# Five pieces instead of three in half-size slots: the down weights of an expert stage's first round

## The chip, the cores and the metric

The kernel runs on one core of a Trainium2 chip. What counts is the device time of one execution in microseconds, taken as the median of several runs. TensorE multiplies matrices, VectorE and ScalarE work on their results, GpSimd does small things, and SyncE (SP) issues the loads from the chip's memory.

## What is computed

The program runs a whole small network on 256 tokens of width 1024 in float32: first two layers of attention and a mixture of experts, then two layers of gated feed-forward blocks around an mLSTM and a Mamba-2 mixer. The change lies in the mixture of experts, which runs once in each of the first two layers. Of the reference, this is what matters:

```python
def _hier_moe(x, w_group, b_group, w_expert, b_expert, w1, w3, w2):
    ...
    order = jnp.argsort(expert_id)        # 16 experts, two of them for each token
    ...
    def expert_block(args):
        xb, e = args
        h = jax.nn.silu(xb @ w1[e]) * (xb @ w3[e])
        return h @ w2[e]

    ys = lax.map(expert_block, (xs, chunk_expert)).reshape(n_slots, d)
    ys = ys * slot_gate[:, None].astype(ys.dtype)
    return jax.ops.segment_sum(ys, slot_tok, num_segments=n_tok + 1)[:n_tok]
```

`w1` and `w3` are 1024 x 512 for each expert, `w2` is 512 x 1024. All 16 experts' weights are loaded, about 100 MB for each layer.

## The kernel before

**Rounds.** The 16 experts are worked in seven rounds (`ROUNDS`: 2, 2, 4, 1, 2, 3 and 2 experts). The first four experts have fixed numbers. The others are taken in the order of how many tokens chose them; `place_sorted` (L1070 to L1091) finds that order on VectorE with two scratch tiles, `flp` and `flx`, writes the expert numbers to `who` (L1090), and SP reads each of them with a TENSOR_LOAD (L1091) before the loads that need it. In round p, `up` multiplies the tokens that `dispatch` gathered into `xe` by `w1` and `w3` (lines "w,xe"), then `h` is the gated result; `down(p)` transposes it to `hT` and multiplies by `w2` (lines "w,hT" or "wh,hT"), and the results, scaled to `yh` and `yl`, are added up (lines "yh,CT" and "yl,CT"). `up(p + 1)` is written ahead of `down(p)`.

**Pieces and slots.** Each expert's weights come in 12 pieces of 512 KB, four each of `w1`, `w3` and `w2`. The generator `experts` (L936) hands them out in the order in which they are used, and every piece takes a slot in the core's memory with `take` and issues its load on SP: L269 for `w1` and `w3` (through `load_w2`), L258 for `w2` (through `load_w`). There are 37 whole slots (`N_UNIT`) and 16 half ones (`N_HALF`). Slots of one size stand in a line: `give` puts a slot at the line's end when the code is through with it, `take` takes the first, both in the order in which the code is written. So a piece's slot, and whoever used that slot last, are fixed when the program is built. The load then has to wait until that last user is done.

**The half slots.** The first `IN_HALVES` pieces of round 0's `w2` don't take one whole slot but two half ones, with a load of 256 KB for each (L955 to L960); `w[0]` holds columns 0 to 511 and `w[1]` the others. In `down`, a product takes the half that it needs:

```python
if name == "w2" and r == 0 and 2 * i + c < IN_HALVES:
    w = [self.take([512], "wh") for _ in range(2)]
    for j in range(2):
        self.nc.sync.dma_start(w[j], A[name][l, c, k * P:(k + 1) * P, j * 512:(j + 1) * 512])
    yield w
else:
    yield piece()
```

Round 0 has experts 0 and 1, and their `w2` pieces alternate: piece 1 is expert 0's first quarter of rows, piece 2 expert 1's, piece 3 expert 0's second quarter, and so on to piece 8. The half slots are also used by `h`, `flp` and other small tiles.

**What sets the order.** The code is written once; a scheduler then places each engine's instructions, by its own estimate of their times. Each engine works through its own list in order, and an instruction that waits holds everything behind it on its engine. SP issues all weight loads of the stage, so a load that waits for its slot holds the loads behind it. Eight loads can be on their way at a time (each takes one of eight semaphores in turn, and waits for the one eight places before).

Of the kernel before, what the change touches and what calls it, by code (L numbers as in the profile page):

```python
# [33 lines left out]
LL0, LL1 = True, True  # L34
KEEP = 14
OVER_UNITS = 6
IN_HALVES = 3
FIXED = 4


# [94 lines left out]
class K:  # L135
# [800 lines left out]
    def experts(self, l):  # L936
# [11 lines left out]
        for r in range(len(ROUNDS) + 1):  # L948
            for name, r, kt, n in (("w1", r, KT, 512), ("w3", r, KT, 512), ("w2", r - 1, 4, D)):
# [3 lines left out]
                for i, pieces in enumerate(zip(*(load(at(name, e), kt) for e in ROUNDS[r]))):  # L953
                    for c, (k, _, piece) in enumerate(pieces):
                        if name == "w2" and r == 0 and 2 * i + c < IN_HALVES:  # L955
                            w = [self.take([512], "wh") for _ in range(2)]
# [1062 lines left out]
```

## Time and profile before

| | us |
|---|---|
| three runs | 2154.83, 2161.49, 2166.03 |
| their median | 2161.49 |
| the profiled execution | 2156.63 |
| its span in the trace | 2154.9 |

| engine | busy, share of the span |
|---|---|
| TensorE | 93% |
| VectorE | 57% |
| ScalarE | 39% |
| GpSimd | 3% |
| transfers (16 engines) | 68.4% |

The profile shows one execution. Its page cuts the span into forty slices of 53.9 us each. An answer on a stretch gives the instructions in order of time, the busy time by engine, or what each engine waited for; L12 is line 12 of the kernel, and times are counted from the start of the span. TensorE's times are partly modelled, so a busy TensorE is not one at its peak. In layer 0 the expert stage lies at about 250 to 470 us, in layer 1 at about 710 to 930.

### The profile page before, as it was taken

Reading aid. Unit: us, or ns where it says so; the run is one execution under the profiler, and the core shown is the slowest. Engines: PE = TensorE matmul, PEld = TensorE weight load, DVE = VectorE, ACT = ScalarE, POOL = GpSimd, SP = SyncE. Lnnn points to the kernel's source line nnn. Section 1 sums busy time; section 2 is a strip of 40 time slices with the busy share of each in tenths; the row PEclk is TensorE's granted clock in tenths of the full one; section 3 lists DMA queues with packets and bytes.
Section 4 is the critical chain, followed back from the end, with each engine's and each line's share of the span. In section 5 each row is a group of like instructions: output and inputs, shape, how many; then the busy total and the mean of one; then the engine's idle time right before and its main releaser. Section 6 shows DMA issues by size and latency. Waiting matters only on the chain.

```text
span 2154.9 us, 28260 instructions
## 1 busy us (share of the span) xinstructions
PE 2009.5 (93%) x10417; PEld 1463.1 (68%) x10417; DVE 1226.0 (57%) x2049; ACT 834.2 (39%) x1359; POOL 63.4 (3%) x108
## 2 busy tenths in 40 slices
PE   7998899989997999979998979999999898998998
PEld 6866543338776443257786867777778797876887
DVE  5876411137776311177657776677667578655544
ACT  5543100024443100054334554345444456745442
POOL 1000000010000000000000000000000000000000
PEclk9998899999998999989998989999999999999999
DMA  6854799986755999968847746874786343334662
GB/s 226 318 160 150 278 410 411 411 335 226 256 176 193 364 409 410 410 207 272 270 161 262 254 147 203 275 261 150 252 281 219 110 129 117 104 136 143 188 209 82
DMA packets 214232, 515.85 MB, mean 239 GB/s; under 512 B 23562, under 2 KB 36936, under 8 KB 214088
## 3 DMA queue, kind: packets, MB, share of 16 engines
q1 hardware_dynamic: 214088, 513.98, 68.4%
q8 instruction: 84, 1.38, 0.3%
q14 instruction: 60, 0.49, 0.1%
HBM read 512.87 MB, written 1.05 MB: 238 GB/s over the span
## 4 chain that ended last, share of the span: by engine, by line
PE 45%; DMA 4%; DVE 4%; ACT 2%; issue 1%; POOL 0%; SPq 0%; DVEq 0%; POOLq 0%; ACTq 0%
PE ps L200 39%; PE ps L122 4%; DMA w<-in_ffn_w_dram 2%; DVE lo L293 2%; PE ps L204 1%; DMA w<-in_mb_w_in_dram 1%; DMA adaw<-in_ada_w_dram 1%; ACT hi L290 1%; DMA w<-in_ml_w_in_dram 1%; DVE xTm L393 0%; DVE lo L297 0%; ACT xTm L395 0%; DVE xTl L398 0%; PE ps L1411 0%; DVE adac L1447 0%
## 5 line engine op out<-in xcount | busy, mean ns | idle before, releaser
L200 PE MATMUL ps<-hi,xTh 128*128 128x512 f32 (+3 forms) x1632 | 641.7, 397 | 38.4 <-ACT xTh L397 24.0
L200 PE MATMUL ps<-hi,xTl 128*128 128x512 f32 (+3 forms) x1632 | 636.3, 390 | 7.5 <-DVE xTl L398 7.2
L293 DVE TENSOR_TENSOR lo<-w,hi 128x1024 fp32r<-128x1024 f32 (+2 forms) x458 | 482.0, 1074 | 271.1 <-ACT hi L290 261.5
L290 ACT CAST hi<-w 128x1024 fp32r<-128x1024 f32 (+2 forms) x458 | 416.3, 931 | 511.4 <-DMA w<-in_ffn_w_dram 331.4
L200 PE MATMUL ps<-lo,xTh 128*128 128x512 f32 (+3 forms) x1632 | 611.1, 387 | 0.9 <-DVE lo L293 0.6
L200 PEld LDWEIGHTS ps<-hi,xTh 128*128 128x128 f32 x1632 | 315.6, 194 | 112.6 <-ACT xTh L397 29.8
L200 PEld LDWEIGHTS ps<-hi,xTl 128*128 128x128 f32 x1632 | 316.8, 194 | 76.9 <-DVE xTl L398 13.6
L200 PEld LDWEIGHTS ps<-lo,xTh 128*128 128x128 f32 x1632 | 313.2, 192 | 66.2 <-DVE lo L293 2.0
L200 PE MATMUL ps<-w,xe 128*32 128x512 f32 (+2 forms) x1088 | 222.8, 597 | 1.7 <-DMA w<-in_w_dram 1.5
L1447 DVE SCALAR_TENSOR_TENSOR adac<-adaw,cact,adac 128x512 f32<-128x512 f32 x252 | 187.4, 748 | 13.8 <-DMA adaw<-in_ada_w_dram 9.8
L200 PEld LDWEIGHTS ps<-w,xe 128*32 128x32 f32 (+2 forms) x1088 | 65.5, 124 | 131.0 <-issue 110.4
L200 PE MATMUL ps<-w,hT 128*32 128x512 f32 (+2 forms) x520 | 132.8, 599 | 0.0
L122 PE MATMUL ps<-xTh,hi 128*128 128x256 f32 x384 | 112.4, 294 | 7.3 <-DVE dr L559 3.5
L122 PE MATMUL ps<-xTh,lo 128*128 128x256 f32 x384 | 111.3, 290 | 0.4 <-DVE lo L293 0.4
L122 PE MATMUL ps<-xTl,hi 128*128 128x256 f32 x384 | 109.9, 288 | 0.0
L1206 DVE TENSOR_TENSOR h<-h,ps 128x512 f32<-128x512 f32 (+1 forms) x14 | 9.6, 687 | 144.9 <-PE ps L200 143.7
L1228 ACT ACTIVATE yh<-ps,gs 128x512 fp32r<-128x512 f32 (+1 forms) x28 | 18.9, 686 | 186.0 <-PE ps L200 185.5
L200 PEld LDWEIGHTS ps<-w,hT 128*32 128x32 f32 (+2 forms) x520 | 38.0, 123 | 72.4 <-issue 59.4
L122 PEld LDWEIGHTS ps<-xTh,hi 128*128 128x128 f32 x384 | 75.2, 197 | 8.9 <-issue 4.0
L397 ACT CAST xTh<-ps 128x512 fp32r<-128x512 f32 (+1 forms) x84 | 42.7, 523 | 92.8 <-PE ps L204 89.7
L1229 DVE SCALAR_TENSOR_TENSOR yl<-ps,gs,yh 128x512 fp32r<-128x512 f32 (+1 forms) x28 | 20.7, 749 | 101.5 <-ACT yh L1228 101.0
L122 PEld LDWEIGHTS ps<-xTh,lo 128*128 128x128 f32 x384 | 75.4, 196 | 0.8 <-DVE lo L293 0.5
(350 smaller groups left out, 2014.2 us busy)
## 6 DMA issues: line engine op xcount, KB each, us to landing
w<-in_w_dram SPq DMA_DIRECT2D x378, 512.0 KB, 10.1
w<-in_ffn_w_dram SPq DMA_DIRECT2D x264, 512.0 KB, 4.6
adaw<-in_ada_w_dram SPq DMA_DIRECT2D x144, 512.0 KB, 4.9
w<-in_w_in_dram SPq DMA_DIRECT2D x60, 512.0 KB, 6.2
w<-in_mb_w_in_dram SPq DMA_DIRECT2D x40, 512.0 KB, 4.2
w<-in_ml_w_in_dram SPq DMA_DIRECT2D x24, 512.0 KB, 5.7
w<-in_w_out_dram SPq DMA_DIRECT2D x16, 512.0 KB, 5.7
w<-in_mb_w_out_dram SPq DMA_DIRECT2D x16, 512.0 KB, 3.3
```

What stands on the lines that cost most here:

```text
L122: self.k.nc.tensor.matmul(out, lhsT, rhs, start=not self.started, stop=stop)
L200: self.nc.tensor.matmul(out, lhsT, rhs, start=start, stop=stop)
L204: self.nc.tensor.transpose(out, in_, self.ident[:n, :n])
L290: self.nc.scalar.copy(hi[:, k], w[:, k])
L293: self.nc.vector.tensor_sub(lo[:, k], w[:, k], hi[:, k].bitcast(F32))
L397: first = nc.scalar.copy(h, ps)
L1206: V.tensor_mul(h[:m], h[:m], hp[1][:m])
L1228: nc.scalar.mul(yh[:m], py[n][:m], g)
L1229: V.scalar_tensor_tensor(yl[:m], py[n][:m], g, yh[:m].bitcast(F32), OP.mult, OP.subtract)
L1447: nc.vector.scalar_tensor_tensor(prev, wt[:, k], cc, prev, OP.mult, OP.add)
```

## The change

One number is changed: `IN_HALVES` is 5. So pieces 4 and 5 of round 0's `w2`, in each of the two layers, take two half slots and two loads of 256 KB each instead of one whole slot and one load.

```diff
 KEEP = 14
 OVER_UNITS = 6
-IN_HALVES = 3
+IN_HALVES = 5
 FIXED = 4
```

By the code's own lines of slots, in layer 0 piece 4's halves now take the slots that `flp` and round 0's `h` had, and piece 5's halves take those of piece 1 (the tiles `wh_2548` and `wh_2549` below). Pieces 6 to 8 and all later ones take other whole slots than before, two places further back in the line. The scheduler places the loads and products anew. In the rows below, a number behind a name tells tiles of one name apart, "x2" stands for two alike, and the names in brackets are semaphores: DMAHW is one of the eight for loads, PE, DVE (VectorE) and Activation (ScalarE) stand for the engine waited for.

**SP ahead of the expert numbers**, layer 0. Before (pieces 4 to 8 are the whole tiles `w_2564`, `w_2570`, `w_2572`, `w_2578` and `w_2580`):

```order
L258 DMA w_2564<-in_w2_dram 128x1024 [waits DMAHW4_49,PE_49]
L258 DMA w_2570<-in_w2_dram 128x1024 [waits DMAHW5_49,PE_49]
L258 DMA w_2578<-in_w2_dram 128x1024 [waits DMAHW6_49,PE_49]
L258 DMA w_2580<-in_w2_dram 128x1024 [waits DMAHW7_49,PE_49]
L258 DMA w_2572<-in_w2_dram 128x1024 [waits DMAHW0_49,DVE_49]
L1091 TENSOR_LOAD who_2368 [waits DVE_49]
L1091 ISA x2
L1091 TENSOR_LOAD who_2368
```

After:

```order
L258 DMA w_2576<-in_w2_dram 128x1024 [waits DMAHW4_49,PE_49]
L258 DMA w_2582<-in_w2_dram 128x1024 [waits DMAHW5_49,PE_49]
L958 DMA wh_2564<-in_w2_dram 128x512 [waits DMAHW6_49,DVE_49]
L258 DMA w_2584<-in_w2_dram 128x1024 [waits DMAHW7_49,DVE_49]
L1091 TENSOR_LOAD who_2368 [waits DVE_49]
L1091 ISA x2
L1091 TENSOR_LOAD who_2368
L1091 ISA x2
```

Pieces 6 to 8 are `w_2576`, `w_2582` and `w_2584` now, and `wh_2564` is piece 4's first half. Two whole loads less and one half more stand ahead of the reads of `who`. After the rows shown, five reads in all stand ahead of the first load of round 2, where four did.

**SP at the end of the loads of round 2's `w1` and `w3`**, layer 0, some 28 loads later. The `w2` pieces here belong to round 1. Before:

```order
L269 DMA w_2800<-in_w3_dram 128x1024 [waits DMAHW6_49,PE_49]
L269 ISA
L269 DMA w_2802<-in_w3_dram 128x1024 [waits DMAHW7_49,PE_49]
L269 ISA
L269 DMA w_2804<-in_w3_dram 128x1024 [waits DMAHW0_49,PE_49]
L258 DMA w_2826<-in_w2_dram 128x1024 [waits DMAHW1_49,PE_49]
L258 DMA w_2828<-in_w2_dram 128x1024 [waits DMAHW2_49,PE_49]
L258 DMA w_2834<-in_w2_dram 128x1024 [waits DMAHW3_49,PE_49]
L258 DMA w_2836<-in_w2_dram 128x1024 [waits DMAHW4_49,PE_49]
```

After:

```order
L958 DMA wh_2565<-in_w2_dram 128x512 [waits DMAHW2_49,DVE_49,PE_49]
L269 ISA
L269 DMA w_2790<-in_w3_dram 128x1024 [waits DMAHW3_49,Activation_49]
L269 ISA
L269 DMA w_2792<-in_w3_dram 128x1024 [waits DMAHW4_49,Activation_49]
L958 DMA wh_2572<-in_w2_dram 128x512 [waits DMAHW5_49,PE_49]
L958 DMA wh_2573<-in_w2_dram 128x512 [waits DMAHW6_49,PE_49]
L269 ISA
L269 DMA w_2802<-in_w3_dram 128x1024 [waits DMAHW7_49,PE_49]
L269 ISA
L269 DMA w_2804<-in_w3_dram 128x1024 [waits DMAHW0_49,PE_49]
```

Three half loads stand here now: piece 4's second half and, two loads later, both halves of piece 5, which wait for TensorE. The load behind them, `w_2802`, takes the slot of `w_2576`, which is piece 6.

**TensorE in the first down step**, layer 0: products of round 0's `hT` with the pieces. Before, from the fourth product on:

```order
L200 MATMUL ps_2547<-wh_2553,hT_2544 64x512
L200 MATMUL ps_2546<-wh_2560,hT_2544 64x512
L200 MATMUL ps_2546<-w_2564,hT_2544 64x512
L200 MATMUL ps_2547<-wh_2561,hT_2544 64x512
L200 MATMUL ps_2547<-w_2564,hT_2544 64x512
L200 MATMUL ps_2546<-w_2570,hT_2544 64x512
L200 MATMUL ps_2546<-w_2572,hT_2544 64x512
L200 MATMUL ps_2547<-w_2570,hT_2544 64x512
L200 MATMUL ps_2547<-w_2572,hT_2544 64x512
L200 MATMUL ps_2546<-w_2578,hT_2544 64x512
L200 MATMUL ps_2546<-w_2580,hT_2544 64x512
L200 MATMUL ps_2547<-w_2578,hT_2544 64x512
```

After, from piece 5 on (the product with piece 4's second half, `wh_2565`, stands seven rows above; ahead of that stand 12 rows of dispatch and the transposes of the next round's `h`, most of which stood behind this down step before):

```order
L122 MATMUL ps_2925<-R_2184,Ds_2259 128x2
L200 MATMUL ps_2546<-wh_2572,hT_2544 64x512
L200 MATMUL ps_2546<-w_2576,hT_2544 64x512
L200 MATMUL ps_2546<-w_2582,hT_2544 64x512
L200 MATMUL ps_2546<-w_2584,hT_2544 64x512
L204 MATMUL ps_2937<-cf_73,Ds_2259 64x128
L204 MATMUL ps_2937<-cf_73,Ds_2259 128x128 x2
L200 MATMUL ps_2547<-wh_2573,hT_2544 64x512
L200 MATMUL ps_2547<-w_2576,hT_2544 64x512
L200 MATMUL ps_2547<-w_2582,hT_2544 64x512
L200 MATMUL ps_2547<-w_2584,hT_2544 64x512
L200 MATMUL ps_2297<-yh_2590,CT_2448 128x512
```

The products with pieces 6 to 8 (`w_2576`, `w_2582`, `w_2584`) stand half behind `wh_2572` and half behind `wh_2573`, so the slot of `w_2576` is free one product after the last half of piece 5 is used. In layer 1 the two lists are changed in the same places.

On SP the order differs besides only among the loads of the mLSTM's weights and of the modulation's (`adaw`), where some change places.

## Rows read from the trace of the kernel before

**Rows 1.** The page's forty slices of 53.9 us: GB/s that the transfer engines moved.

```profile
GB/s 226 318 160 150 278 410 411 411 335 226 256 176 193 364 409 410 410 207 272 270 161 262 254 147 203 275 261 150 252 281 219 110 129 117 104 136 143 188 209 82
```

**Rows 2.** Both stages' windows: engines' busy us (count), PEclk, DMA share, GB/s.

```profile
255.00:260.00 5.00, 5.00 (x28) 2.35 (x28) 3.09 (x8) 0.00 (x0) 0.00 (x0) 1.00 1.01 336
260.00:265.00 5.00, 5.00 (x26) 1.72 (x24) 3.89 (x17) 0.32 (x1) 0.00 (x0) 1.00 0.94 340
265.00:270.00 5.00, 5.00 (x34) 2.87 (x30) 1.29 (x5) 2.15 (x3) 0.00 (x0) 1.00 0.94 332
...
420.00:460.00 40.00, 39.03 (x154) 10.94 (x156) 3.36 (x5) 1.97 (x3) 3.12 (x6) 1.00 1.03 411
...
850.00:900.00 50.00, 48.85 (x248) 15.55 (x248) 6.54 (x11) 2.83 (x5) 0.00 (x0) 1.00 1.03 410
```

**Rows 3.** SP in order, 250 to 330: start, duration, load, count.

```profile
254.68 6.56 SPq L258 DMA_DIRECT2D w<-in_w_dram  x5
264.07 35.23 SPq L269 DMA_DIRECT2D w<-in_w_dram  x32
300.19 9.29 SPq L258 DMA_DIRECT2D w<-in_w_dram  x8
310.49 9.08 SPq L269 DMA_DIRECT2D w<-in_w_dram  x8
```

**Rows 4.** What SP waited for, 300 to 466: total, times, longest, us.

```profile
SPq L269 <- DMA w<-in_w_dram: 48.2, 64, 1.4
SPq L258 <- DMA w<-in_w_dram: 45.4, 61, 1.4
```

**Rows 5.** What TensorE's weight loads waited for, 400 to 466.

```profile
PEld ps L200 <- DMA w<-in_w_dram: 9.6, 21, 1.2
PEld ps L200 <- ACT yh L1228: 2.9, 4, 0.8
```

**Rows 6.** VectorE in order, 255 to 263: the sorting's last steps.

```profile
258.74 1.06 DVE L1086 TENSOR_TENSOR flx<-R,flp 128x864 f32<-128x864 f32 x1
...
260.92 0.16 DVE L1090 CAST who<-R 1x12 int32<-1x12 f32 x1
```

**Rows 7.** SP's reads of the expert numbers: count, ns, first and last start.

```profile
L1091 SPq TENSOR_LOAD <-who x12: 263/268/469, 261.3 to 275.9; - x12
```

**Rows 8.** The page's list of loads: count, KB, median us to landing.

```profile
w<-in_w_dram SPq DMA_DIRECT2D x378, 512.0 KB, 10.1
```

**Rows 9.** TensorE in order, 266 to 300: first down step, round 2's start.

```profile
286.30 2.33 PE L200 MATMUL ps<-wh,hT 128*64 128x512 f32 x9
...
289.37 4.03 PE L200 MATMUL ps<-w,hT 128*64 128x512 f32 x17
293.32 0.51 PE L122 MATMUL ps<-Ds,xh 128*128 128x256 f32 x2
...
295.35 0.62 PE L200 MATMUL ps<-yh,CT 128*128 128x512 f32 x2
...
296.37 1.90 PE L200 MATMUL ps<-w,xe 128*32 128x512 f32 x10
```

**Rows 10.** Loads into an empty queue, issued at 216.6 and 235.7.

```profile
DMA to landing us min/median/max: 3.5/3.5/3.5
...
DMA to landing us min/median/max: 3.6/3.6/3.6
```

**Rows 11.** SP in order in layer 1, 705 to 790.

```profile
712.21 4.44 SPq L258 DMA_DIRECT2D w<-in_w_dram  x5
...
756.17 9.92 SPq L258 DMA_DIRECT2D w<-in_w_dram  x8
```

**Rows 12.** What ScalarE waited for, 1129 to 1260.

```profile
ACT hi L290 <- DMA w<-in_ml_w_in_dram: 29.7, 17, 7.6
```

**Rows 13.** What SP waited for, 250 to 300.

```profile
SPq L269 <- PE ps L200: 8.0, 7, 5.8
SPq L258 <- PE ps L200: 4.0, 2, 3.1
```

## The prediction

> **What bounds the kernel now.** I read the forty slices of the page first. In [rows 1] the line of GB/s stands at 409 to 411 in slices 6 to 8 and 15 to 17 (each 53.9 us wide), and nowhere else. Those are the two expert stages, one for each layer. The windows [rows 2] give both the same picture: about 410 GB/s with a DMA share above 1. The transfer queue is full there, and one 512 KB piece takes 524288 B / 411 GB/s = 1.28 us of it. [rows 3] agree: eight loads issued over 9.29 us, and the next of them 10.3 us after the first (300.19 to 310.49), that is 1.28 us each.
>
> Is the queue the limit, or TensorE, which is shown nearly always busy? Two views decide. SyncE (SP), which issues every load, waits between 300 and 466 us for earlier loads to land: 48.2 and 45.4 us on its two lines [rows 4]. So it has free slots, and only the queue holds it back. TensorE's weight loads wait 9.6 us for arriving weights in the last 66 us of the stage [rows 5]: there it runs directly behind the queue. Whatever leaves the queue empty before that moves the end of the stage by as much. TensorE may be late in the first half without cost, since it catches up.
>
> **What the change removes, adds and moves.** No byte is added. In each layer the fourth and the fifth piece of round 0's down weights (512 KB each) become two loads of 256 KB into half-size slots. Two whole slots are freed, four half slots are taken, all later slots rotate by two, and the scheduler orders the loads anew. The orders shown above tell what matters: the fourth piece's two halves are parted (one ahead of the expert numbers, one 26 loads later), and the fifth stands near the end of the 32 loads for round 2's `w1` and `w3`. The reason is in the slots. The fifth piece gets the two half slots that the first piece held, so these loads have to wait for the first products of the down step.
>
> First term: the start of the stage. Before, five whole loads go out ahead of the expert numbers, in 254.68 to 261.2 [rows 3]. Afterwards it is three whole loads and one half. That half waits for the slot of `flp`, whose last reader is VectorE's L1086, 258.74 + 1.06 = 259.80 [rows 6]; VectorE is not held up by it. Nothing is queued on SP between about 255.5 and 260, and 1.5 units (768 KB) are missing that were issued around 258.6 before. The expert numbers themselves don't come earlier: `who` is written at 260.92 [rows 6], and its first read by SP is at 261.3 [rows 7]. A fifth read stands ahead of the first load that uses one; before, four of them lie between 261.3 and 264.07, 0.7 us each. So the queue falls behind by at most 1.5 x 1.28 + 0.7 = 2.6 us. The lower bound: the queue was not full there before either. It ran at 336, 340 and 332 GB/s from 255 to 270 [rows 2], 15 us x (1 - 336/411) = 2.7 us of idle queue, and the reordered loads may fall into some of it; then 0.5 us remain. I take 2.0, nearer the upper end, because the hole falls where there were transfers and nothing can be issued in it.
>
> Second term: the end of those 32 loads. Afterwards the last half of the fifth piece is directly followed on SP by a load that needs the slot of the sixth piece. TensorE gives that slot back only after it has used the fifth piece. SP issues in order, so it stands there, and behind it stand all later loads of the stage. Call T the time at which that last half lands. Before, the load at this place was issued four loads ahead of 300.19, at 295.1; with 2 us of delay and a landing time of 10.1 us [rows 8], T is about 306 (305 to 308). TensorE has nothing left by then: its seven half products end at about 289.3 [rows 9], and what the scheduler moved ahead of the rest (four more rows of dispatch at 0.24 us, transposes and gate products of the next group) lasts to about 293. From there it waits for weights.
>
> From T on, step by step. The sixteen products of this down step last 7.0 us (286.30 to 293.32, [rows 9]), 0.44 each. The four products that need the first half of the fifth piece begin 0.64 us before T, half a unit. They end at T + 1.1; three transposes take it to T + 1.4; two more products end at T + 2.3, and the sixth piece is used up. About 0.4 us for the semaphore and the issue makes T + 2.7. By then the queue has been empty since T, because all loads behind it are held. A load into an empty queue takes 3.5 or 3.6 us to land [rows 10], so the next piece lands at T + 6.2 where it would have landed at T + 1.28. That is **4.9 us** of lost queue. The two slots behind come free at T + 3.2. The fourth needs round 2's first products: down ends at T + 3.2; a wait for ScalarE's `yh` has taken 0.8 us [rows 5], and its products take 1.0 (295.35 to 296.37, [rows 9]), so round 2 starts at T + 5.0. It gives its first slot back after five products (x10 in the row, each being recorded twice), 1.9 us, at T + 6.9. That load lands at about T + 10.8, where it would have followed its predecessor (T + 8.8) at T + 10.1. After that round 2 frees four slots in eight products, 2.9 us, against 5.1 us of queue for four loads, so the queue stays full. That adds 0.7, and I take 5.6, with bounds of 3.7 (issue at T + 1.5, were the slot free after the first of its two uses) and 7.5 (round 2 gives its slots back 2 us later still).
>
> In layer 1 the orders differ in the same way, and its rows before are the same with other times: five loads at 712.21, eight at 756.17 [rows 11]. So the stage costs 2.0 + 5.6 = 7.6 us, twice: 15.2.
>
> TensorE starts round 2 some 15 us later than 296.37, but has done about 3 us of work ahead by then. It is thus about 12 us late against a queue that is 7.6 us late. That costs nothing more as long as it still catches up before the last 40 us; before, it was waiting for weights in the whole last part [rows 5].
>
> Third term: the rest of the program. On SP only the stretch of the mLSTM's loads is reordered (about 1150 to 1250 us), where `ada` loads and mLSTM weights change places. ScalarE waits 29.7 us in 17 waits for these weights [rows 12], 1.7 us each; a place or two in the order is 1.3 to 2.6 us, to either side. I take 0, with bounds of -3 and +4.
>
> [...] In the full queue a landing every 1.28 us for 512 KB shows no price for a transfer as such, so the two additional ones per layer cost 0 here. [...]
>
> **The sum.** 15.2 us on the profiled execution's own 2156.6 us is 2171.8. That execution lies 4.9 us under the median of the three runs; against the median 2161.5 it is 2176.7, and I say 2176.
>
> **The rivals.** (a) *The freed slots let the stream run ahead*: on the other side. SP waits 12 us for products to give slots back from 250 to 300 us [rows 13]; two slots more could let two loads go 2 x 1.28 us earlier in the idle 2.7 us at 255 to 270. That is -2.6 per layer, 2156. It decides if loads fill the hole before 261.3 and the fifth piece's halves do not hold SP. Against it: the loads that could use the slots need `who`, and the order shows no whole load moved ahead of it. (b) *The block is covered*: eight loads in flight last 10 us, and if TensorE used up the sixth piece before the last half lands, the queue would not run dry, leaving 2 x 2.0, 2165.5. Against it: that piece is used behind the half in TensorE's own order. (c) *TensorE's delay doesn't heal*: slots come back late for another 3 to 6 us per layer, or the 12 us are not made up: 2 x 5 more, 2186. For it: TensorE is shown busy nearly all the time; against it, the catching up in [rows 5]. (d) *Each half pays its transfer's own time*: 3.5 - 1.28 = 2.2 us for each of the four additional loads, 8.8 more, 2185. [...]
>
> **How the numbers follow.** Chances: forecast 0.64, (a) 0.08, (b) 0.12, (c) 0.12, (d) 0.04. The forecast's own range adds its bounds: 2 x (0.5 + 3.7) - 3 to 2 x (2.6 + 7.5) + 4, that is +5 to +24, or 2167 to 2186. The range that holds 8 in 10 goes down to 2161, under (b) and its noise, and up to 2189, over (c). About 0.5%, 10.8 us, is what a measurement of this kernel can tell from no change: 2150.7 to 2172.3. Of the forecast's 0.64 I put 0.18 below 2172.3. So slower is 0.46 + 0.12 + 0.04 = 0.62, within 0.5% is 0.18 + 0.12 + 0.05 = 0.35, and faster is 0.03 of (a).
>
> **What would show it.** Right: in both layers SP stands for about 12 us waiting for TensorE between the last half load and the next; the queue's GB/s falls for 5 to 6 us near 307 and near 763; TensorE waits about 10 us before that for the fourth and fifth piece; the stages end 7 to 8 us later each. The first term shows as a hole in the transfers at 256 to 261. Wrong: GB/s stays at 410 over 300 to 320 (then (b)), the time per layer is the same but the last third of the program has moved (the third term), or transfers above 411 GB/s before 270 (then (a)).

## The result and the profile after

| | before | after |
|---|---|---|
| median, us | 2154.88 (19 runs, 2147.75 to 2166.45) | 2175.34 (19 runs, 2164.59 to 2180.72) |
| the profiled execution's span, us | 2154.9 | 2177.0 |

The changed kernel is slower: the ratio of the times is 1.0081, with a 95% interval of 1.0069 to 1.0094. That is 17.5 us of 2154.88 (14.9 to 20.3); the two medians themselves lie 20.5 us apart. The forecast was 2176, and 15.2 us more than before.

The line of GB/s of the changed kernel's page, forty slices, against [rows 1]:

```profile
GB/s 223 317 157 156 283 311 412 411 364 198 294 142 196 304 331 412 410 308 242 280 242 162 276 205 198 266 263 169 237 276 231 110 129 114 98 136 134 193 199 92
```

Slice 6 (about 270 to 325 us) fell from 410 to 311, and in layer 1 the slices before 412 fell from 364 and 409 to 304 and 331. Slices 9 and 18 are the stages' ends, which came later. The two stages lost what the full queue would have moved.

SP in order in the changed kernel, layer 0 (start, duration, load, count), against [rows 3]; `wh` are the half slots:

```profile
252.62 0.81 SPq L258 DMA_DIRECT2D w<-in_w_dram  x2
257.77 0.33 SPq L958 DMA_DIRECT2D wh<-in_w_dram  x1
258.86 0.33 SPq L258 DMA_DIRECT2D w<-in_w_dram  x1
262.58 27.99 SPq L269 DMA_DIRECT2D w<-in_w_dram  x26
291.49 0.34 SPq L958 DMA_DIRECT2D wh<-in_w_dram  x1
292.81 1.61 SPq L269 DMA_DIRECT2D w<-in_w_dram  x2
295.28 1.64 SPq L958 DMA_DIRECT2D wh<-in_w_dram  x2
312.09 4.14 SPq L269 DMA_DIRECT2D w<-in_w_dram  x4
316.33 6.50 SPq L258 DMA_DIRECT2D w<-in_w_dram  x8
```

The fifth piece's halves are issued until 296.9, and then nothing until 312.09. SP's waits in the changed kernel, 250 to 320 (total, times, longest, us), against [rows 13]:

```profile
SPq L269 <- PE ps L200: 23.4, 7, 14.2
SPq L958 <- DVE flx L1086: 4.3, 1, 4.3
```

One wait for TensorE lasted 14.2 us: the load behind the fifth piece, which needs the sixth piece's slot. The 4.3 us is the fourth piece's first half, waiting for `flx` to have read `flp`. In layer 1 SP does the same:

```profile
771.86 1.57 SPq L958 DMA_DIRECT2D wh<-in_w_dram  x2
787.76 4.14 SPq L269 DMA_DIRECT2D w<-in_w_dram  x4
```

The same stretches by windows, in the changed kernel (span, busy us of PE, PEld, DVE, ACT, POOL with counts, granted clock, DMA share, GB/s), against [rows 2]:

```profile
256.00:261.00 5.00, 5.00 (x26) 1.66 (x24) 4.82 (x15) 0.00 (x0) 0.00 (x0) 1.00 0.68 240
261.00:266.00 5.00, 5.00 (x28) 2.09 (x25) 1.59 (x7) 1.88 (x2) 0.00 (x0) 1.00 0.66 238
...
290.00:300.00 10.00, 2.04 (x16) 1.53 (x15) 0.69 (x1) 0.59 (x1) 0.00 (x0) 0.72 1.03 413
301.00:306.00 5.00, 4.22 (x14) 2.50 (x14) 0.69 (x1) 0.00 (x0) 0.00 (x0) 0.50 0.33 126
306.00:311.00 5.00, 5.00 (x15) 1.64 (x16) 1.41 (x8) 0.69 (x1) 0.00 (x0) 0.50 0.00 0
311.00:316.00 5.00, 5.00 (x32) 1.64 (x32) 1.17 (x2) 0.69 (x1) 0.00 (x0) 0.96 0.40 124
```

The two holes can be weighed as bytes. Over the twenty microseconds from 301 to 321 the changed kernel moved 134 GB/s, where the full queue moves 410:

```profile
301.00:321.00 20.00, 19.22 (x93) 7.49 (x97) 3.84 (x12) 2.12 (x4) 0.00 (x0) 0.74 0.39 134
```

276 GB/s x 20 us is 5.5 MB, at 410 GB/s **13.5 us** of queue. The hole ahead of the expert numbers lies 2 us earlier in this execution than in that of before, so 251 to 271 after stands against 253 to 273 before. The first row is after's, the second before's:

```profile
251.00:271.00 20.00, 20.00 (x104) 8.51 (x102) 9.06 (x34) 2.47 (x3) 0.00 (x0) 1.00 0.80 269
```

```profile
253.00:273.00 20.00, 20.00 (x104) 8.51 (x102) 9.06 (x34) 2.47 (x3) 0.00 (x0) 1.00 0.92 319
```

50 GB/s x 20 us is 1.0 MB, or **2.4 us**. Together 15.9. The same count in layer 1 gives 10.7 us (264 GB/s over 773 to 803) and 2.9 us (247 GB/s over 727.4 to 747.4 after, 306 over 708 to 728 before), 13.6 together. The bytes can be checked against a lag: pair each VectorE instruction with the same one of the profile before (line, kind and tiles alike, counted in order), and take the median difference of their starts in stretches of 10 us. From 270 to 480 us this lag grows by 15.8 us, of which 13.0 are there by 360; over layer 1's stage it grows by 10.8. So the bytes tell the lag to some 3 us. The table gives it for all kernels below, in us, by stretches of before's time; the last column is the ratio of times with its interval, against runs of the kernel before on the same chip.

| kernel | stage 0 (270 to 480) | between the stages (480 to 720) | stage 1 (720 to 930) | mLSTM (1110 to 1300) | ratio of times |
|---|---|---|---|---|---|
| the change | +15.8 | +5.7 | +10.8 | -12.5 | 1.0081 [1.0069, 1.0094] |
| the change again | +13.7 | +2.4 | +12.2 | -10.1 | 1.0070 [1.0047, 1.0093] |
| before again | 0.0 | +2.1 | -0.6 | -1.8 | (one run) |
| five in layer 0 | +11.1 | +4.6 | -2.4 | -5.5 | 1.0046 [1.0024, 1.0067] |
| five in layer 1 | -0.3 | +1.4 | +13.0 | -2.1 | 1.0046 [1.0022, 1.0069] |
| four | +0.5 | +3.8 | -0.3 | -7.1 | 0.9987 [0.9973, 1.0001] |
| five, line turned | +11.1 | +1.1 | +11.5 | -5.5 | 1.0129 [1.0101, 1.0157] |
| three, line turned | -0.3 | +4.8 | -1.5 | -0.8 | 0.9988 [0.9969, 1.0006] |
| five, two more half slots | +0.7 | +15.1 | -1.4 | -4.1 | 0.9997 [0.9985, 1.0009] |
| 34 products more | +23.5 | +6.0 | +22.0 | -5.8 | 1.0174 [1.0147, 1.0200] |
| 19 products more | +17.3 | +4.1 | +13.8 | -7.8 | 1.0128 [1.0100, 1.0157] |
| halves issued by ScalarE | +10.7 | +5.2 | +8.9 | -12.5 | 1.0072 [1.0049, 1.0094] |
| halves issued by GpSimd | +2.2 | +2.5 | +1.4 | -7.1 | 1.0002 [0.9983, 1.0021] |

The kernel before, run again, and the stages that a kernel left alone (0.0 to -2.4), show how far the lag of one execution can be read: to some 2 us in the stages. Between the stages it is less sure (+15.1 in the kernel with two more half slots, whose timed runs show no loss; its profiled execution was the longest of its ten, 2168.70 against a median of 2155.75). So the stages carry the argument; for the rest the times decide.

### The profile page after: what moved, and what is told of

It is laid out like the page before. It is cut to its first block, busy times and chain, and to the rows that moved or that the text cites. A ratio compares the mean times of both kernels' runs of the same rounds, so it can differ in the third digit from the quotient of the medians.

```text
span 2177.0 us, 28244 instructions
## 1 busy us (share of the span) xinstructions
PE 2018.8 (93%) x10417; PEld 1466.1 (67%) x10417; DVE 1225.2 (56%) x2049; ACT 833.1 (38%) x1359; POOL 65.4 (3%) x108
## 5 line engine op out<-in xcount | busy, mean ns | idle before, releaser
L1447 DVE SCALAR_TENSOR_TENSOR adac<-adaw,cact,adac 128x512 f32<-128x512 f32 x252 | 187.8, 749 | 11.1 <-DMA adaw<-in_ada_w_dram 7.2
L122 PEld LDWEIGHTS ps<-xTl,hi 128*128 128x128 f32 x384 | 76.4, 200 | 0.6 <-issue 0.5
```

The source lines that it names most:

```text
L122: self.k.nc.tensor.matmul(out, lhsT, rhs, start=not self.started, stop=stop)
L1447: nc.vector.scalar_tensor_tensor(prev, wt[:, k], cc, prev, OP.mult, OP.add)
```

## The experiments

**One layer at a time, and four pieces.** Are the stages the whole cost, and does each cost the same? The kernel before was run once more beside them, and the change once more later on.

```diff
-IN_HALVES = 3
+IN_HALVES = (5, 3)     # or (3, 5), or (4, 4)
-if name == "w2" and r == 0 and 2 * i + c < IN_HALVES:
+if name == "w2" and r == 0 and 2 * i + c < IN_HALVES[l]:
```

Five in layer 0:

> Five pieces in half slots in layer 0 only, three in layer 1. Theory: the loss is the wait of SP behind the fifth piece's halves, stage by stage. Then layer 0's stage ends about 14 us later than before, with GB/s at 0 around 305 to 310 and SP standing 14 us, and layer 1's stage is as long as before (lag unchanged through it within 1 us). Rival: the change costs through the rotation of all later slots; then layer 1 loses too. The total is +14 less what the mLSTM's stage gives back: its loads stand in a third order here, so 0 to -11.

Five in layer 1:

> Five pieces in half slots in layer 1 only. Theory: layer 0 is as before to the microsecond or two, layer 1's stage ends 11 us later than before, again with 14 us of SP standing. Rival (slot rotation): nothing is lost in the stage itself. Total +11 less what the mLSTM's stage gives back, 0 to -11, with its loads in a fourth order.

Four in both:

> Four pieces in half slots, in both layers. The fourth piece's second half is late here too, but SP has 2 loads with free slots behind it, and TensorE's order puts the other columns' products and round 2's first ones ahead of the product with this half, so SP's slots come free without it. Theory (the block on SP is the price): no stretch with the queue empty near 300, at most 1 to 3 us per stage from the hole ahead of the expert numbers; total -2 to +6 by the stages. Rival (each half load or each late half costs): about half of the change's loss, 6 us per stage, 12 in all.

The kernel before again:

> The kernel before, profiled once more. It sets what two executions of one program differ by, stretch by stretch. If the 11 us that the changed kernel won back in the mLSTM's stage (its lag fell from 29.7 us at 1130 us to 18.5 at 1250) is an accident of one execution, this profile is allowed to differ from the first one by as much there; if it comes from the order of the loads, this one agrees with the first within 2 us over that stage, and the whole span within 6 us.

The change again:

> The changed kernel once more. Theory: layer 0's stage loses 11 to 16 us, layer 1's 11 to 13, and the lag falls by 8 to 12 us over the mLSTM's stage, as in the first profile; total +16 to +22. If the fall in the mLSTM's stage is below 5 here, the first profile's was for the most part an accident, and the time of the run with the other order of these loads (+25.8) has another cause.

Each layer alone costs 0.46% (9.9 us), and its lag grows in its own stage alone: +11.1 and +13.0, against -2.4 and -0.3 in the other. With four pieces nothing is lost, 0.9987. There the fourth piece's second half is issued late too, at 288.20, and SP's longest wait for TensorE on the loads of `w1` and `w3` is 3.2 us. So the late fourth piece by itself costs nothing; what costs is the fifth, at its place on SP.

**The lines of slots turned.** In the change the mLSTM's loads are ordered anew as well. To have the change's stages without that order, the line of half slots was turned by a few places after the second stage, in a kernel with five and in one with three; their orders among the mLSTM's loads are then alike.

```diff
         for n in range(start, min(10, upto)):
+            if n == 4:
+                k.free[HALF].rotate(1)     # five pieces; rotate(3) with three
             k.modulate(host.get(n, []))
```

With five:

> The change, with the line of half slots turned by one place after the second expert stage. The loads of both expert stages stand as in the change; the mLSTM's loads now stand nearly as in the kernel before (runs of modulation and mLSTM loads of one to three, not the runs of six and seven of the change). Theory: the 11 to 12 us that the change won back in the mLSTM's stage come from that order; here they are missing, its lag over 1110 to 1290 us (times of before) changes by less than 3 us, and the program takes about 10 us longer than the change, +26 to +31 on before. Rival: it is an accident, or comes from being late as such; then the lag falls by 10 here too and the time is that of the change, +17 to +20.

With three:

> The kernel before, with the line of half slots turned by three places after the second expert stage, which gives its mLSTM loads the same order as in the run above. Theory: the same as before within 4 us, since this order is nearly before's own; the difference to the run above is then what the two expert stages (and layer 1's attention between them) cost, 26 to 31. Rival: if turning slots as such costs in the last 900 us, both runs show it there.

Three, turned, costs nothing (0.9988). Five, turned, costs 1.29%, 27.8 us (21.8 to 33.9): more than the change itself, by about 10 us and outside its interval. It has four runs, and the profiled one is the shortest of them (2171.47, the others 2178.74 to 2188.54), so its trace does not hold the whole 27.8. The lag of its two stages is 22.6, no more than the change's 26.6 and 25.9. So the change's stages seem to cost more than its time tells, and something later to give part of it back. In the lag it is the mLSTM, though with the line turned the lag falls there by 5.5 and not by less than 3 as expected. Three kernels have the change's load order there, load for load: the change, its repeat, and the one with halves issued by ScalarE. In these the lag falls by 12.5, 10.1 and 12.5; in the ten others, none of which has this order, by 0.8 to 7.8, 4.8 in the mean. The difference of the means is 7 us. It is not that a late program catches up by itself: the kernel with 34 products more comes there 48 us late and makes up 5.8.

A part of it can be read in ScalarE's waits for these weights (total, times, longest), 1110 to 1290: the first fence is the changed kernel, the second five with the line turned, against 29.7 in [rows 12]:

```profile
ACT hi L290 <- DMA w<-in_ml_w_in_dram: 22.1, 12, 6.5
```

```profile
ACT hi L290 <- DMA w<-in_ml_w_in_dram: 28.8, 13, 8.0
```

Some 7 us less wait with the change's order, and hardly less with the other. But the total does not tell the orders apart: the two kernels with additional products, described below, have 22.1 as well, without that order, and with a fall of the lag by no more than 5.8 and 7.8. The longest single wait does: 6.5, 6.5 and 6.8 in the three kernels with the change's order, 7.2 to 8.5 in the eleven others, before's two profiles included. A kernel with before's stages and the change's order in the mLSTM wasn't run. So this gain is not shown by itself, its cause is argued, and why the scheduler orders the loads so there is open.

**Two more half slots.** The line of half slots is made 18 long (and that of whole ones 36), so that the fifth piece's halves no longer come back to the first piece's slots. The four additional loads stay.

```diff
-N_UNIT, N_HALF = 37, 16
+N_UNIT, N_HALF = 36, 18
-IN_HALVES = 3
+IN_HALVES = (5, 5)
```

> Five pieces in half slots, but with 18 half slots and 36 whole ones. Piece 5 no longer takes the slots of piece 1, and only its second half stands late, with the ring of whole slots free behind it. Theory (SP's block by the reused slots is the price): no empty queue near 305, the expert stages as long as before within 2 us each, so the loss of 26 vanishes; total -6 to +4, the mLSTM's loads being in yet another order. Rival (five pieces in ten loads of 256 KB cost as such, or 4 half loads more): still 5 or more per stage.

0.9997: nothing is lost. The same pieces are cut in the same halves, so the number of loads costs nothing that can be measured; it was the place of the waiting halves.

**Products that keep TensorE busy.** TensorE's granted clock fell to 0.50 in the changed kernel (301 to 311), after it had waited 8.6 us for the fourth piece's half. To have the clock up, products whose result nobody reads were put behind the second group of round 0's down step, first 34, then 19. They are additional work; nothing is left out.

```diff
+if p == 0 and k == 1:
+    junk = self.ps_tr()
+    for i in range(34):     # then 19
+        self.mm(junk[:64], hT[:, 0, :64], w[0][0], i == 0, i == 34 - 1)
 give(w)
```

34:

> The change, with 34 additional products of 64 x 512 (0.44 us each at the full clock, into a bank that nobody reads) behind the seventh product of the first down step, in both layers; they keep TensorE at work from about 288 to 303 us while it would wait for the late halves. The gate products that stood between piece 4's and piece 5's products now stand behind them. Theory: of the 13 us that the queue stands empty, 5 come from TensorE's granted clock, which had fallen to 0.50 when the halves landed (products with the late pieces 0.9 us apart in place of 0.44), and 2 more from the gate products in between; so the clock stays at 1.00 here, SP issues again at about 306 and not at 312, and each stage loses 5 to 8 us less: 10 to 15 in all. Rival: the landing and the number of products set it, the clock only looks bad; then SP issues at 310 or later and nothing is won.

19:

> The change with 19 additional products in place of the 34 of the earlier run, which took 0.78 us each and ended 13 us too late (its products with the late pieces then followed each other at 0.43 us, and SP issued 2.8 us after the first). 19 of them end about when the late halves land, near 300 to 301. Theory: SP issues within 3 to 4 us of that, at about 304, the granted clock stays at 1.00, and the stage loses 8 to 9 us, as the prediction worked it out (7.6), in place of 12 to 16; total +14 to +20 (its mLSTM loads stand near before's order, so without the gain there). Rival: the clock is not what made the difference; then SP issues at 308 or later and the stages cost 11 or more each, total +24.

Neither gained, and the times that the two rivals gave came true, but for another reason than theirs. TensorE's list with 34 (the first row holds them all, the rows behind it are products with the late pieces), then a window in which SP stands, and SP's next issue:

```profile
281.85 32.37 PE L200 MATMUL ps<-wh,hT 128*64 128x512 f32 x83 [0.96 <-DVE hT L1216]
313.64 0.64 PE L200 MATMUL ps<-w,hT 128*64 128x512 f32 x1
314.06 0.59 PE L200 MATMUL ps<-wh,hT 128*64 128x512 f32 x1
```

```profile
305.00:310.00 5.00, 5.00 (x15) 1.70 (x14) 0.00 (x0) 0.00 (x0) 0.00 (x0) 1.00 0.00 0
```

```profile
316.42 7.86 SPq L269 DMA_DIRECT2D w<-in_w_dram  x4
```

The clock stays at 1.00, and from the first product with late pieces at 313.64 to SP's issue at 316.42 it is 2.8 us, against 5.9 in the changed kernel, whose products stand in another order. But the 34 took 0.78 us each where 0.44 was expected (why is open), and reach past the landing of the halves, so the stage ends later still. With 19 they end at 303.43; dispatch and the product with the fourth piece's half stand behind them, then twelve more rows of dispatch, so the fifth piece's products begin at 308.79, and SP issues at 312.37, as late as without. So the products with the late pieces follow each other at 0.42 us with 1.00 granted (313.64, 314.06) and at 0.9 with 0.50, but neither kernel shows what a stage would gain from the clock alone.

**Another engine issues the late halves.** The halves of pieces 4 and 5 are issued by ScalarE, or by GpSimd. Slots are the change's, and TensorE's order of the late products nearly so.

```diff
-self.nc.sync.dma_start(w[j], ...)
+(self.nc.sync if 2 * i + c < 3 else self.nc.scalar).dma_start(w[j], ...)   # or self.nc.gpsimd
```

By ScalarE:

> The change, with the loads of pieces 4 and 5 (four halves in each layer) issued by ScalarE instead of SP. Slots, TensorE's products in the first down step and the mLSTM's loads stand as in the change. Theory: the price of the stages is the place of the late halves on SP, behind 26 loads and ahead of all the rest; issued from another engine they leave when their slots come free (about 286 to 292 us) and land by about 300, TensorE waits 0 to 5 us and SP stands less than 5; what remains per stage is the hole ahead of the expert numbers, 2 us, and up to 4 more. The mLSTM's stage gives back 8 to 12 as in the change. Total -8 to +4, most likely -3, so the version may beat both. Rival: the reused slots themselves are the price (the halves must wait for piece 1 in any queue); then the stages cost 10 or more each here too.

By GpSimd:

> The same with GpSimd as the issuing engine, and with the mLSTM's loads in an order near before's, so without the 8 to 12 us there. Theory: stages as in the run above, 2 to 6 us each; total +2 to +10. Rival as above: +20 or more.

By ScalarE it costs 0.72%, like the change; the expected -8 to +4 us missed, and the stages cost about the rival's 10 (10.7 and 8.9). ScalarE's list (ACTq are its load issues):

```profile
271.80 0.60 ACT L1205 ACTIVATE h<-ps 128x512 f32<-128x512 f32 x1 [9.03 <-PE ps L200]
286.30 0.34 ACTq L958 DMA_DIRECT2D wh<-in_w_dram  x1
286.67 0.59 ACT L230 COPY xe<-ps 128x512 f32<-128x512 f32 x1 [14.28 <-DMA w<-in_w_dram]
290.08 2.07 ACTq L958 DMA_DIRECT2D wh<-in_w_dram  x2
```

The load waited for its slot until 286.30, and behind it on ScalarE stood the copies of the next round's tokens. Not all of the 14.28 us ahead of the first copy is the load's: in the changed kernel and in the one with GpSimd the same copy stands 7.82 us behind its `h`. So the load held it by some 6.5 us. TensorE waited 2.4 and 2.0 us for the copies, its clock fell to 0.50 and then 0.61, and SP stood 11.4 us for it:

```profile
295.00:300.00 5.00, 4.22 (x17) 2.82 (x18) 1.59 (x7) 0.00 (x0) 0.00 (x0) 0.50 0.63 246
300.00:305.00 5.00, 5.00 (x19) 1.33 (x15) 0.93 (x3) 0.69 (x1) 0.00 (x0) 0.61 0.00 0
```

In this kernel the halves themselves did not come late: TensorE began with the fifth piece at 298.93, none of its waits over 250 to 330 was for a half, and from 300 to 305 nothing was left to move (0 GB/s). It was TensorE that came late, and SP waited for the sixth piece's slot all the same.

By GpSimd the loss is gone, 1.0002, though this kernel's mLSTM loads are not in the change's order. GpSimd's issues, then SP's list and its waits (250 to 320), and the window 305 to 310, in most of which the changed kernel had no transfer:

```profile
284.08 0.55 POOL L958 DMA_DIRECT2D wh<-in_w_dram  x1 [1.43 <-PE ps L200]
284.94 0.55 POOL L958 DMA_DIRECT2D wh<-in_w_dram  x1 [0.31 <-issue]
```

```profile
260.81 40.23 SPq L269 DMA_DIRECT2D w<-in_w_dram  x32
```

```profile
SPq L269 <- PE ps L200: 6.8, 9, 2.3
```

```profile
305.00:310.00 5.00, 5.00 (x52) 1.56 (x48) 0.28 (x1) 0.70 (x2) 0.00 (x0) 1.00 1.03 411
```

The fifth piece's halves go out at 284.08 and 284.94, as soon as TensorE has given back the first piece's slots, some 9 us earlier than in the changed kernel (295.28, in an execution whose first down step begins 1.8 us later). They land before TensorE comes to them, and SP waits no longer than 2.3 us for TensorE. With the same slots nothing stalls for long; so the reuse of the first piece's slots isn't the cause by itself. The cause is the place on SP's one list: far back, so the halves come late, and right ahead of a load that only their products can release. The kernel with ScalarE shows that another delay of TensorE ahead of the sixth piece has the same effect. What is left in the stages, +2.2 and +1.4, is of the size of the first term, and no larger than the lag can be read.

The change and the kernel with GpSimd load the same pieces into the same slots, and their times differ by 0.7 to 0.8%. That is more than SP's issuing of the eight halves, 0.33 us each or 2.6 in all: a load that waits holds its engine's list, SP's by 14.2 us in the change, and ScalarE's copy by 6.5 us.

## Why the prediction was right, and where its terms were not

**The time and the sign.** 2176 stands against 2175.34, but part of that is luck. The base was 6.6 us too high (the median of three runs, 2161.49, against 2154.88 of nineteen), and the increase too low, 15.2 against 17.5 by the ratio and 20.5 by the medians. That increase is itself two misses that offset each other: the two stages cost some 11 us more than forecast (26.6 and 25.9 in the lag, against 15.2), and the mLSTM gave, by estimate, about 7 back where 0 was taken.

**What bounds the kernel.** Right. A hole of 5.5 MB in the queue came out at the end of the stage as lag, and TensorE, 17.6 us late at round 2's start (313.96 against 296.37), waited for weights again in the stage's last part. TensorE's weight loads in the changed kernel, 400 to 480, against [rows 5]:

```profile
PEld ps L200 <- DMA w<-in_w_dram: 12.7, 26, 1.2
```

So one half of rival (c), that TensorE's delay isn't made up, fell. Its other half came: slots came back later than forecast, and the stages cost some 5 us more each, as (c) priced it. The total stayed near the forecast because of the two other misses named above.

**First term, 2.0 us a stage.** About right: 2.4 us by the bytes in layer 0 and 2.9 in layer 1, where the upper bound was 2.6; the hole lies at 256 to 266, and SP waits for `flx` as forecast. The kernel with GpSimd, which keeps this hole and not the other, has +2.2 and +1.4.

**Second term, 5.6 us a stage (3.7 to 7.5).** The mechanism was right, the size was not: 13.5 us by the bytes in layer 0. T, the landing of the fifth piece's last half, was about right: issued at 296.57, it landed 8.1 us later, at 304.7; the forecast was 306, in an execution whose stage began 2 us later. (The queue's bytes had ended some 2 us before that: 126 GB/s over the five microseconds from 301 are 1.5 us of full queue.) The forecast had SP issue at T + 2.7 and that load land at T + 6.2. SP issued at 312.09, T + 7.4, and the load landed 3.8 us later, at T + 11.2. The two times to landing, first of the last half, then of the load at 312.09:

```profile
DMA to landing us min/median/max: 8.1/8.1/8.1
...
DMA to landing us min/median/max: 3.8/3.8/3.8
```

TensorE's list in the changed kernel shows where the 4.7 us until SP's issue lie:

```profile
291.84 0.55 PE L204 MATMUL ps<-cf,Ds 128*128 128x128 f32 x3 [0.35 <-DVE xe L230]
300.98 1.97 PE L200 MATMUL ps<-wh,hT 128*64 128x512 f32 x2 [8.60 <-DMA wh<-in_w_dram]
303.74 2.48 PE L122 MATMUL ps<-R,Ds 128*128 128x2 f32 x12 [0.78 <-DVE hT L1216]
306.15 1.11 PE L200 MATMUL ps<-wh,hT 128*64 128x512 f32 x1
...
307.06 2.76 PE L200 MATMUL ps<-w,hT 128*64 128x512 f32 x5
309.76 0.85 PE L204 MATMUL ps<-cf,Ds 128*64 128x128 f32 x3
310.54 1.08 PE L200 MATMUL ps<-wh,hT 128*64 128x512 f32 x1
```

The forecast's "TensorE has nothing left by then" did not hold. TensorE waited from 292.4 to 300.98 for the fourth piece's late half. Behind that half's product stood, in its own order, a wait for `hT` and the twelve gate products, which the forecast let be done by 293, and only then the fifth piece. So the fifth piece's products began at 306.15, T + 1.45, and not at T - 0.64: 2.1 us. From there to SP's issue it took 5.9 us and not 3.3: 2.6 us.

Nearly all of this is TensorE's clock. After 8.6 us of waiting the granted clock is 0.50 until 311, and products stand 0.9 us apart (306.15, 307.06) where the forecast took 0.44 from [rows 9]. The kernel with GpSimd runs nearly the same list at 1.00; its window, TensorE's rows and SP's next issue:

```profile
290.00:300.00 10.00, 9.14 (x52) 4.22 (x56) 3.30 (x11) 1.37 (x2) 0.00 (x0) 1.00 1.03 410
```

```profile
290.55 1.07 PE L200 MATMUL ps<-wh,hT 128*64 128x512 f32 x2
292.41 1.47 PE L122 MATMUL ps<-R,Ds 128*128 128x2 f32 x12 [0.78 <-DVE hT L1216]
293.81 0.64 PE L200 MATMUL ps<-wh,hT 128*64 128x512 f32 x1
```

```profile
296.64 0.33 SPq L269 DMA_DIRECT2D w<-in_w_dram  x1
```

From the first product with the fourth piece's half to SP's issue it is 6.1 us there (290.55 to 296.64) and 11.1 in the changed kernel (300.98 to 312.09). At most 0.8 of the difference are the three transposes of 309.76, which stand elsewhere in the other list. With the steps of the kernel with GpSimd, SP would have issued at 307 to 308, about the forecast's T + 2.7. This is an estimate: no run has the change's loads with 1.00 granted and in this order. So the step that failed is the price of TensorE's steps around T: 0.44 us each, as read where 1.00 was granted (286 to 293 in before). The prediction said nothing of the clock, though it had TensorE wait for 10 us.

After that landing the queue lost some 3 us more until it was full, where the forecast had 0.7; the cause of that is open. In layer 1 the stage's lag is 10.8 and 12.2 in the two profiles of the change, and 13.0 with that layer alone.

**Third term, 0 (-3 to +4).** Wrong, as far as the runs tell: about -7, outside its bounds, by the difference of the means above, and some -10 by the two ratios, 1.0129 and 1.0081. The forecast priced a place or two in the order by the mean wait, 1.7 us. But the waits there are uneven, 7.6 us in the longest, and a new order of many loads can take more than the mean from several of them. The bound should have come from the longest waits on the reordered loads.

**The other rivals.** (a), the stream running ahead, fell: over 251 to 271 fewer bytes moved, not more. (b), a covered block, fell in the change, and is what the kernel with GpSimd does: its halves land before they are needed. (d), that each half pays its own transfer, fell by the kernel with two more half slots, which has the same four additional loads and a ratio of 0.9997, as far as this queue with eight loads on their way goes.

None of the kernels run is faster than before beyond its interval. One with GpSimd's issues or the two more half slots, and the change's load order in the mLSTM, wasn't tried.

## What to carry to other kernels

Where one engine issues all loads in order, ask of each load moved what has to happen before it may go, and whether that in turn waits for a load just ahead of it. Such a loop emptied the whole queue here for as long as the consumer needed (0 GB/s over 306 to 311), and the consumer's steps have to be counted from its own list, with all that stands between, and at the clock that it has after waiting (0.50 here, after 8.6 us). If a late load has to stay, let an engine with nothing else to do issue it (GpSimd here, 1.0002; ScalarE, which had copies to make, 1.0072).

## What the runs showed of the hardware

TensorE's clock fell just where the stall was: granted 0.50 over 301 to 311, after 8.6 us in which TensorE waited, and products 0.9 us apart instead of 0.44. So the stall that one late load began was made longer by the slower work that followed the wait: 11.1 us for nearly the same list that took 6.1 with 1.00 granted. In the kernel with 34 products more TensorE was busy through that time (5.00 us of the 5 from 305), and 1.00 was granted. Cutting 512 KB loads into halves cost nothing in a queue with eight on their way (0.9997 with four more loads).
